# Opening each ConvFFN of a two-layer decoder trunk with one pair of column tiles instead of two

## The chip, the cores and the metric

The kernel runs on one core of a Trainium2 chip, as one launch. The metric is the device time of one execution in microseconds; the median of three runs is given. The engines are TensorE (PE, with its weight loads as PEld), VectorE (DVE), ScalarE (ACT), GpSimd (POOL) and SyncE (SP), which here issues the DMAs.

## The reference

A hybrid decoder trunk of two layers on an input of 256 rows by 1024 columns, float32. Layer 0 adds an mLSTM mixer, layer 1 a block-sparse attention over a shared K and V; each layer then adds a ConvFFN, and this is what the change touches:

```python
def conv_ffn(x, norm_g, w_up, conv_w, conv_b, w_down):
    s_ = x.shape[1]
    u = rmsnorm(x, norm_g) @ w_up                 # 1024 -> 2 * 2816
    up = jnp.pad(u, ((0, 0), (CONV_W - 1, 0), (0, 0)))
    c = conv_b + up[:, 0:s_] * conv_w[0]
    for j in range(1, CONV_W):                    # three taps along the sequence
        c = c + up[:, j:j + s_] * conv_w[j]
    val, gate = jnp.split(c, 2, axis=-1)
    return (jax.nn.silu(gate) * val) @ w_down

# each layer:  h = h + mixer(h);  h = h + conv_ffn(h, ...)
# rmsnorm(x, g) = x * rsqrt(mean(x * x) + 1e-6) * g
```

## The kernel before

The activations are held transposed: hT is eight tiles of 128 columns of the model by 256 rows of the sequence. Each float32 product is built from high and low parts: a weight unit of 128 x 2048 is loaded by SP into raw (three buffers), copied by ACT into hi and subtracted by DVE into lo, in two halves each (`unit`, L164 to L174; hi and lo have four buffers each). The operands are split alike; `xa` holds the gain-scaled tiles of hT, high part and low part side by side.

A step of `steps_w` (L227) is one slice k of 128 model columns into one column tile of the output: one matmul of the unit's low part on the operand's high part (256 columns, L246), and one of the unit's high part on both parts of the operand (512 columns, L242). The result stands in one of five PSUM accumulators (`acc`); it has two halves of 256 columns, which `whole` (L279) adds together with an ACT copy and a DVE addition.

What runs before a ConvFFN is `project_out` (L298): eight output tiles n, and with the last step of each, `residual` (L289) adds both halves of the accumulator to hT[n] (L290, L292) and `feed` splits hT[n] into xa[n] (L181 on ACT, L182 on DVE) and adds its squares to `sqacc` (L199 on ACT, L200 on POOL, for the last tile on DVE). So the operands of the ConvFFN appear one by one, and the sum of squares behind the last.

The up projection has 22 pairs of column tiles: pair i is the value tile and the gate tile i, and has one weight unit, so 16 steps. The normalisation factor of a row is not known before all eight tiles of hT are. Pairs 0 to 2 (`DEFER`) therefore run on the unnormalised operand xa and are multiplied by the factor afterwards; from pair 3 on the operand is xb, which `rescale` builds from hT and the factor: for each k a product xs on DVE (L349, four buffers), its high part on ACT (L351) and its low part on POOL (L352). `Rstd.sums` adds sqacc over the partitions on PE (L213), then DVE and POOL make the factor (L215, L217); `Rstd.row`, the first thing in `rescale`, spreads it over the partitions by two PE transposes (L222) and an ACT copy into rB (L224).

PE's instructions keep the order in which they are written. The other engines' are put in order by a planner as their operands and buffers come free. `mix` (L69) writes PE steps in their order and puts an item between them as soon as the steps before it have a summed cost of at least the item's number; a step counts 0.32:

```python
def mix(steps, items=()):
    items, now = list(items), 0.0
    for cost, step in steps:
        while items and items[0][0] <= now:
            items.pop(0)[1]()
        step()
        now += cost
```

Before, the opening mixes pairs 0 and 1: for each k, four steps, two for each pair. The sums (5.0) stand after 16 of its 32 steps, the rescaling (6.6) after 21. Then `finish(0)` and `finish(1)` evacuate both pairs, convolve (L323, L327, L330) and gate them, and from pair 2 on each pair runs its 16 steps (all k of one half, then of the other) and is finished.

Of the kernel before, what the change touches and what calls it, by code (L numbers as in the profile page):

```python
# [21 lines left out]
KD = D // P  # L22
NT = S // P
FF = 2816
KF = FF // P
# [8 lines left out]
BIG = 1e30  # L34
L = 2
DEFER = 3
AHEAD = 2
GROUP = 4
HOLD = 4
WARM = 8  # L40
# [28 lines left out]
# [8 lines that stand above are left out]
    for _, item in items:  # L77
        item()
# [3 lines left out]
def yoco_kernel(ctx: ExitStack, tc: tile.TileContext, A, out):  # L82
# [23 lines left out]
    for j in range(4):  # L106
        c = slice(j * 512, (j + 1) * 512)
        nc.sync.dma_start(raw0[:, c], A["w_kq"][0, :, c])
        if j < 3:
            k = slice(2 * j + 2, 2 * j + 4)  # L110
# [16 lines left out]
    for j in range(WARM):  # L127
        ps = pmis.tile([P, 512], F32, name="mis")
# [35 lines left out]
    def unit(src, length, raw=None, pieces=PIECES):  # L164
        if raw is None:
            raw = wraw.tile([P, 2048], F32, name="raw")[:, :length]
            nc.sync.dma_start(raw, src)
        hi = wsp.tile([P, 2048], F32R, name="hi")[:, :length]
        lo = wsp.tile([P, 2048], F32R, name="lo")[:, :length]
        for j in range(pieces):  # L170
            c = slice(j * length // pieces, (j + 1) * length // pieces)
            nc.scalar.activation(hi[:, c], raw[:, c], AF.Copy)  # L172
            nc.vector.tensor_tensor(lo[:, c], raw[:, c], hi[:, c].bitcast(F32), OP.subtract)  # L173
        return hi, lo  # L174
# [11 lines left out]
    def operand(pool, name, n):  # L186
        ts = [pool.tile([P, 2 * S], F32R, name=f"{name}{k}") for k in range(n)]
        return [t[:, :S] for t in ts], [t[:, S:] for t in ts], ts
# [38 lines left out]
    def steps_w(ps, w, at, x, ks, kall, done=None, apart=True):  # L227


        xh, xl, both = x  # L230

        def one(k):
            (hi, lo), p = w(), ps()
            c = slice(at(k), at(k) + P)
            last = k == kall - 1

            def high():
                if not apart:
                    for n, xs in enumerate((xh, xl)):
                        nc.tensor.matmul(p[:, :S], hi[:, c], xs[k], start=k == 0 and n == 0, stop=last and n == 1)  # L240
                    return
                nc.tensor.matmul(p, hi[:, c], both[k], start=k == 0, stop=last)  # L242

            if k == 0:
                high()
            nc.tensor.matmul(p[:, :S], lo[:, c], xh[k], start=False, stop=False)  # L246
            if k > 0:
                high()
            if last and done is not None:
                done(p)  # L250

        return [(0.32, lambda k=k: one(k)) for k in ks]
# [26 lines left out]
    def whole(ps, rows=P):  # L279

        y = work.tile([P, S], F32, name="whole", bufs=WHOLE)[:rows]
        nc.scalar.activation(y, ps[:rows, S:], AF.Copy)  # L282
        nc.vector.tensor_tensor(y, ps[:rows, :S], y, OP.add)  # L283
        return y
# [4 lines left out]
    def residual(n, ps, gains, apart=True):  # L289
        nc.vector.tensor_tensor(hT[:, n], ps[:, :S], hT[:, n], OP.add)  # L290
        if apart:
            nc.vector.tensor_tensor(hT[:, n], ps[:, S:], hT[:, n], OP.add)  # L292
        if gains is None:
            nc.sync.dma_start(out[:, n, :], hT[:, n])
        else:
            feed(n, gains)
# [16 lines left out]
    def conv_ffn(l, gains):  # L313
        r = Rstd()
        with tc.tile_pool(name=f"ffn{l}", bufs=1, reuse_waits="tile") as fp, \
                tc.tile_pool(name=f"ffw{l}", bufs=2, reuse_waits="tile") as fw:
            act = operand(fp, "f", KF)
            ah, al, _ = act

            def conv(ps, c, scaled):  # L320
                u = whole(ps)
                if not scaled:
                    nc.vector.tensor_tensor(u, u, r.rB, OP.mult)  # L323
                w = [par[:, C_CW + (l * 3 + j) * 2 * KF + c:][:, :1] for j in range(3)]
                b = par[:, C_CB + l * 2 * KF + c:][:, :1]
                y = fw.tile([P, S], F32, name="y", bufs=4)
                nc.scalar.activation(y, u, AF.Identity, bias=b, scale=w[2])  # L327
                for j in (1, 0):
                    d = 2 - j
                    nc.vector.scalar_tensor_tensor(y[:, d:], u[:, :S - d], w[j], y[:, d:],  # L330
                                                   op0=OP.mult, op1=OP.add)
                return y

            def finish(i, ps):
                y = [conv(ps[half](), half * KF + i, i >= DEFER) for half in range(2)]
                sg = fw.tile([P, S], F32, name="sg", bufs=2)
                nc.scalar.activation(sg, y[1], AF.Silu)  # L337
                a = fw.tile([P, S], F32, name="a", bufs=2)
                nc.gpsimd.tensor_tensor(out=a, in0=sg, in1=y[0], op=OP.mult)  # L339
                nc.scalar.activation(ah[i], a, AF.Copy)  # L340
                nc.gpsimd.tensor_tensor(out=al[i], in0=a, in1=ah[i].bitcast(F32), op=OP.subtract)  # L341

            def rescale():

                r.row()
                g0 = C_FNORM + l * KD
                for k in range(KD):
                    xs = fw.tile([P, S], F32, name="xs", bufs=4)
                    nc.vector.scalar_tensor_tensor(xs, hT[:, k], par[:, g0 + k:g0 + k + 1], r.rB,  # L349
                                                   op0=OP.mult, op1=OP.mult)  # L350
                    nc.scalar.activation(setB[0][k], xs, AF.Copy)  # L351
                    nc.gpsimd.tensor_tensor(out=setB[1][k], in0=xs, in1=setB[0][k].bitcast(F32), op=OP.subtract)  # L352

            def pair(i, ks):
                x = setA if i < DEFER else setB
                return [s for half in range(2)
                        for s in steps_w(ps[i][half], w[i], lambda k, half=half: k * 256 + half * P, x, ks, KD)]

            w = [Once(lambda i=i: unit(A["w_up"][l, i], 2048)) for i in range(KF)]
            ps = [[Once(acc) for half in range(2)] for i in range(KF)]  # L360

            mix([s for k in range(KD) for i in range(AHEAD) for s in pair_k(pair, i, k)],
                [(5.0, r.sums), (6.6, rescale)])
            for i in range(AHEAD):
                finish(i, ps[i])
            for i in range(AHEAD, KF):
                mix(pair(i, range(KD)))
                finish(i, ps[i])

            wd = [Once(lambda i=i: unit(A["w_down"][l, i], 11 * P)) for i in range(2 * KD)]  # L370
            pd = [Once(acc) for n in range(KD)]

            def down(n, ks):
                apart = gains is not None or n < KD - 1
                return [s for k in ks for s in
                        steps_w(pd[n], wd[2 * n + k // 11], lambda q: (q % 11) * P, act, [k], KF,
                                lambda p: residual(n, p, gains, apart), apart)]


            for ks in (range(KF // 2), range(KF // 2, KF)):  # L380
                for n in range(HOLD):
                    mix(down(n, ks))
            for n in range(HOLD, KD):
                mix(down(n, range(KF)))

    def pair_k(pair, i, k):
        return pair(i, [k])


    wgv = wgs.rearrange("p (k m) -> p k m", k=KD)  # L390
# [12 lines left out]
    with tc.tile_pool(name="mls", bufs=1, reuse_waits="tile") as mp, \  # L403
            tc.tile_pool(name="mlw", bufs=2, reuse_waits="tile") as mw:
        r = Rstd()
# [199 lines left out]
    for i in range(2):  # L605
# [3 lines left out]
        for a in range(2):  # L609
            ha, hb = slice(a * HALF, (a + 1) * HALF), slice((1 - a) * HALF, (2 - a) * HALF)  # L610
            nc.gpsimd.tensor_tensor(out=tab[:, i, :, 1, ha], in0=rope[:, :, 1, ha], op=OP.mult,  # L611
                                    in1=g[:, None, hb].to_broadcast([P, NT, HALF]))

    conv_ffn(0, [(C_KVNORM, setA), (C_BNORM, setB)])


    with tc.tile_pool(name="att", bufs=1, reuse_waits="tile") as mp, \
            tc.tile_pool(name="atw", bufs=2, reuse_waits="tile") as mw:
        r = Rstd()
# [105 lines left out]
        project_out(A["w_o"], setB, [(C_FNORM + KD, setA)], [it(1.0 + 0.6 * h, values, 4 + h) for h in range(4)])  # L725

    conv_ffn(1, None)


# [68 lines left out]
```

## Time and profile before

| what | value |
|---|---|
| median of 3 runs | 602.32 us (602.27 to 602.56) |
| the profiled execution's own time | 602.21 us |
| its span, first to last instruction | 600.5 us |
| PE busy in the span | 591.0 us (98%) |
| DVE busy | 495.4 us (82%) |
| ACT busy | 393.0 us (65%) |
| POOL busy | 172.7 us (29%) |
| mean granted TensorE clock | 0.996 of full speed |

The profile is of one execution. Its span leaves out what lies before the first and behind the last instruction, 1.7 us here. Busy is the time in which an engine has an instruction under way; matmuls overlap, and their ends are modelled, so the starts are what counts for PE. The first ConvFFN starts at about 115.9 us of the span, the second at about 410.2 us.

### The profile page before, as it was taken

How to read it: one execution, taken by the hardware profiler on the slowest of the kernel's cores; microseconds unless marked ns; L12 is line 12 of the kernel's file. 1: busy time of each engine (PE TensorE's matmuls, PEld its weight loads, DVE VectorE, ACT ScalarE, POOL GpSimd, SP SyncE). 2: the span in 40 equal slices, each digit the busy share in tenths (PEclk: the TensorE clock that was granted, in tenths of full speed). 3: DMA queues.
4: the chain of work that ended last, by engine and by line, in shares of the span. 5: the costliest groups of instructions: out<-in, count | busy, mean ns of one | idle time of the engine just before them, and what ended most of it. 6: DMA issues, size and time to landing. Idle time of an engine off the chain costs nothing.

```text
span 600.5 us, 8992 instructions
## 1 busy us (share of the span) xinstructions
PE 591.0 (98%) x3278; PEld 504.8 (84%) x3278; DVE 495.4 (82%) x837; ACT 393.0 (65%) x713; POOL 172.7 (29%) x186
## 2 busy tenths in 40 slices
PE   7899999999999999999999999999999999999997
PEld 4787888888888888888888878888888888888887
DVE  7897677979999999988768786467999999998650
ACT  5756776667886777765656687554878767676430
POOL 6600310343545344301111200022545453432000
PEclk8999999999999999999999999999999999999999
DMA  7874434617445543486755533335364456346830
GB/s 245 309 269 181 141 140 141 211 70 255 167 151 200 199 139 136 151 266 203 246 204 185 200 120 139 129 138 214 106 228 158 153 198 209 103 141 209 265 110 19
DMA packets 18621, 105.79 MB, mean 176 GB/s; under 512 B 2320, under 2 KB 3856, under 8 KB 9104
## 3 DMA queue, kind: packets, MB, share of 16 engines
q1 hardware_dynamic: 18576, 105.21, 50.0%
q8 instruction: 26, 0.43, 0.3%
q14 instruction: 19, 0.16, 0.1%
HBM read 104.15 MB, written 1.05 MB: 175 GB/s over the span
## 4 chain that ended last, share of the span: by engine, by line
PE 87%; DVE 6%; ACT 3%; POOL 2%; issue 1%; DMA 1%; SPq 0%; DVEq 0%; POOLq 0%
PE acc L242 41%; PE acc L246 21%; PE acc L263 6%; PE acc L265 6%; PE acc L264 6%; DVE lo L173 3%; ACT hi L172 1%; DVE xs L349 1%; DVE xa L182 1%; PE acc L240 1%; DMA hT<-xT 1%; PE mis L551 1%; POOL tab L611 1%; DVE hT L292 1%; PE mis L666 1%
## 5 line engine op out<-in xcount | busy, mean ns | idle before, releaser
L173 DVE TENSOR_TENSOR lo<-raw,hi 128x1024 fp32r<-128x1024 f32 (+2 forms) x218 | 247.5, 1165 | 28.9 <-ACT hi L172 28.6
L242 PE MATMUL acc<-xb,hi 128*128 128x512 f32 x736 | 252.3, 396 | 0.6 <-POOL xb L352 0.6
L172 ACT ACTIVATE hi<-raw 128x1024 fp32r<-128x1024 f32 (+2 forms) x218 | 199.8, 964 | 56.1 <-PE acc L242 25.4
L246 PE MATMUL acc<-xb,lo 128*128 128x256 f32 x736 | 191.3, 279 | 0.0
L242 PEld LDWEIGHTS acc<-xb,hi 128*128 128x128 f32 x736 | 131.8, 188 | 26.2 <-POOL xb L352 1.2
L246 PEld LDWEIGHTS acc<-xb,lo 128*128 128x128 f32 x736 | 138.7, 188 | 8.0
L242 PE MATMUL acc<-f,hi 128*128 128x512 f32 x330 | 115.0, 394 | 0.0
L330 DVE SCALAR_TENSOR_TENSOR y<-whole,par,y 128x254 f32<-128x254 f32 (+1 forms) x176 | 110.2, 645 | 3.2 <-ACT y L327 2.8
L246 PE MATMUL acc<-f,lo 128*128 128x256 f32 x352 | 96.8, 282 | 0.0
L339 POOL TENSOR_TENSOR a<-sg,y 128x256 f32<-128x256 f32 x44 | 58.7, 1333 | 97.6 <-ACT sg L337 97.6
L242 PEld LDWEIGHTS acc<-f,hi 128*128 128x128 f32 x330 | 61.1, 188 | 13.0
L246 PEld LDWEIGHTS acc<-f,lo 128*128 128x128 f32 x352 | 66.1, 188 | 1.3
L327 ACT ACTIVATE y<-whole,par 128x256 f32<-128x256 f32 x88 | 51.7, 595 | 20.8 <-DVE whole L283 18.8
L242 PE MATMUL acc<-xa,hi 128*128 128x512 f32 x160 | 57.4, 402 | 0.9 <-DVE hT L292 0.5
L263 PE MATMUL acc<-hi,xa 128*128 128x512 f32 x128 | 53.3, 417 | 0.0
L341 POOL TENSOR_TENSOR f<-a,f 128x256 fp32r<-128x256 f32 x44 | 42.3, 962 | 36.3 <-ACT f L340 36.3
L265 PE MATMUL acc<-hi,xa 128*128 128x512 f32 x128 | 50.1, 391 | 0.0
L264 PE MATMUL acc<-lo,xa 128*128 128x512 f32 x128 | 50.0, 391 | 0.0
L200 POOL TENSOR_TENSOR sqacc<-sqacc,sq 128x256 f32<-128x256 f32 x18 | 16.4, 910 | 115.2 <-ACT sq L199 115.2
L246 PE MATMUL acc<-xa,lo 128*128 128x256 f32 x160 | 44.3, 289 | 0.5 <-DVE lo L173 0.5
L283 DVE TENSOR_TENSOR whole<-acc,whole 128x256 f32<-128x256 f32 (+1 forms) x97 | 39.4, 412 | 0.0
L282 ACT ACTIVATE whole<-acc 128x256 f32<-128x256 f32 (+1 forms) x97 | 35.4, 368 | 5.8 <-PE acc L242 5.7
(180 smaller groups left out, 638.2 us busy)
## 6 DMA issues: line engine op xcount, KB each, us to landing
raw<-w_up SPq DMA_DIRECT2D x44, 1024.0 KB, 4.8
raw<-w_down SPq DMA_DIRECT2D x32, 704.0 KB, 4.7
raw<-w_kqv SPq DMA_DIRECT2D x12, 1024.0 KB, 4.8
raw<-w_vo SPq DMA_DIRECT2D x8, 1024.0 KB, 4.9
raw<-w_out SPq DMA_DIRECT2D x4, 1024.0 KB, 4.9
raw<-w_o SPq DMA_DIRECT2D x4, 1024.0 KB, 4.8
raw<-w_kq SPq DMA_DIRECT2D x2, 1024.0 KB, 7.8
raw<-w_kq SPq DMA_DIRECT2D x4, 256.0 KB, 5.4
```

The lines of the kernel that those rows point to most:

```text
L172: nc.scalar.activation(hi[:, c], raw[:, c], AF.Copy)
L173: nc.vector.tensor_tensor(lo[:, c], raw[:, c], hi[:, c].bitcast(F32), OP.subtract)
L242: nc.tensor.matmul(p, hi[:, c], both[k], start=k == 0, stop=last)
L246: nc.tensor.matmul(p[:, :S], lo[:, c], xh[k], start=False, stop=False)
L263: nc.tensor.matmul(p, xh[k][:, ts], hi[:, c], start=k == 0, stop=False)
L264: nc.tensor.matmul(p, xh[k][:, ts], lo[:, c], start=False, stop=False)
L265: nc.tensor.matmul(p, xl[k][:, ts], hi[:, c], start=False, stop=k == KD - 1)
L283: nc.vector.tensor_tensor(y, ps[:rows, :S], y, OP.add)
L327: nc.scalar.activation(y, u, AF.Identity, bias=b, scale=w[2])
L330: nc.vector.scalar_tensor_tensor(y[:, d:], u[:, :S - d], w[j], y[:, d:], op0=OP.mult, op1=OP.add)
L339: nc.gpsimd.tensor_tensor(out=a, in0=sg, in1=y[0], op=OP.mult)
L341: nc.gpsimd.tensor_tensor(out=al[i], in0=a, in1=ah[i].bitcast(F32), op=OP.subtract)
```

## The change

The opening takes pair 0 alone, slice by slice: two steps for each k. The sums stand after 14 of these 16 steps. Pair 1 runs behind them, one half after the other as later pairs do, with the rescaling after three of its steps. The constant AHEAD and the function `pair_k` go; everything else stays.

```diff
-AHEAD = 2
...
-            mix([s for k in range(KD) for i in range(AHEAD) for s in pair_k(pair, i, k)],
-                [(5.0, r.sums), (6.6, rescale)])
-            for i in range(AHEAD):
-                finish(i, ps[i])
-            for i in range(AHEAD, KF):
-                mix(pair(i, range(KD)))
+            mix([s for k in range(KD) for s in pair(0, [k])], [(4.2, r.sums)])
+            mix(pair(1, range(KD)), [(0.7, rescale)])
+            for i in range(KF):
+                if i > 1:
+                    mix(pair(i, range(KD)))
                 finish(i, ps[i])
...
-    def pair_k(pair, i, k):
-        return pair(i, [k])
```

## Rows read from the trace of the kernel before

**Rows 1.** The page, part 1: busy time, share, instructions of PE.

```profile
PE 591.0 (98%) x3278; PEld 504.8 (84%) x3278; DVE 495.4 (82%) x837; ACT 393.0 (65%) x713; POOL 172.7 (29%) x186
```

**Rows 2.** Waits of PE, whole span: us in total, times, longest us.

```profile
PE acc L242 <- POOL xb L352: 0.6, 2, 0.3
PE acc L242 <- DVE hT L292: 0.5, 2, 0.3
```

**Rows 3.** Timeline of PE, first opening: start us, us, what, idle time before and releaser.

```profile
115.89 0.40 PE L242 MATMUL acc<-xa,hi 128*128 128x512 f32 x1
...
117.37 0.47 PE L242 MATMUL acc<-xa,hi 128*128 128x512 f32 x1 [0.27 <-DVE hT L292]
...
118.27 0.39 PE L242 MATMUL acc<-xa,hi 128*128 128x512 f32 x1
...
121.73 0.39 PE L242 MATMUL acc<-xa,hi 128*128 128x512 f32 x1
122.01 0.61 PE L213 MATMUL mis<-tri,sqacc 128*128 128x1 f32 x4
122.47 0.37 PE L246 MATMUL acc<-xa,lo 128*128 128x256 f32 x1
...
124.30 0.38 PE L222 MATMUL mis<-ident,rc 128*128 128x128 f32 x2
```

**Rows 4.** Timeline of ACT, first opening.

```profile
116.09 2.01 ACT L172 ACTIVATE hi<-raw 128x1024 fp32r<-128x1024 f32 x2 [1.30 <-PE acc L242]
118.00 0.49 ACT L181 ACTIVATE xa<-hT,par 128x256 fp32r<-128x256 f32 x1
...
118.71 0.49 ACT L181 ACTIVATE xa<-hT,par 128x256 fp32r<-128x256 f32 x1
...
124.72 0.39 ACT L224 ACTIVATE rB<-mis 128x256 f32<-128x256 f32 x1 [5.20 <-PE mis L222]
```

**Rows 5.** Timeline of DVE, first opening.

```profile
117.93 2.90 DVE L173 TENSOR_TENSOR lo<-raw,hi 128x1024 fp32r<-128x1024 f32 x2
120.75 0.87 DVE L182 SCALAR_TENSOR_TENSOR xa<-hT,par,xa 128x256 fp32r<-128x256 f32 x2
121.54 0.41 DVE L200 TENSOR_TENSOR sqacc<-sqacc,sq 128x256 f32<-128x256 f32 x1
...
125.14 3.93 DVE L349 SCALAR_TENSOR_TENSOR xs<-hT,par,rB 128x256 f32<-128x256 f32 x6 [2.33 <-ACT rB L224]
```

**Rows 6.** Chain that ended last, from rescaling to pair 3: start us, us, what.

```profile
128.91 1.89 ACT hi L172 x2
130.80 0.28 ACT whole L282
...
131.66 1.90 ACT hi L172 x2
...
133.85 0.98 ACT y L327 x2
...
135.22 1.72 POOL xb L352
```

**Rows 7.** Timeline of PE, eighth step of pair 3, first and second ConvFFN.

```profile
136.98 0.72 PE L242 MATMUL acc<-xb,hi 128*128 128x512 f32 x2 [0.33 <-POOL xb L352]
...
431.33 0.73 PE L242 MATMUL acc<-xb,hi 128*128 128x512 f32 x2 [0.29 <-POOL xb L352]
```

**Rows 8.** Timelines of POOL and DVE, first rescaling.

```profile
126.15 4.22 POOL L352 TENSOR_TENSOR xb<-xs,xb 128x256 fp32r<-128x256 f32 x5 [2.55 <-ACT xb L351]
...
135.13 2.88 DVE L173 TENSOR_TENSOR lo<-raw,hi 128x1024 fp32r<-128x1024 f32 x2
```

**Rows 9.** Stretch after the rescaling: us, busy us of engines, PE clock, DMA share, GB/s.

```profile
137.00:240.00 103.00, 103.00 (x589) 89.77 (x590) 101.32 (x156) 76.96 (x147) 45.45 (x38) 1.00 0.50 178
```

**Rows 10.** Timeline of DVE, second opening.

```profile
412.29 2.90 DVE L173 TENSOR_TENSOR lo<-raw,hi 128x1024 fp32r<-128x1024 f32 x2
415.11 0.87 DVE L182 SCALAR_TENSOR_TENSOR xa<-hT,par,xa 128x256 fp32r<-128x256 f32 x2
```

## Prediction

> **What bounds the kernel now.** I read the page first: PE is busy for 591.0 of 600.5 us [rows 1], so only a PE wait that comes or goes can move the end. Then PE's waits: in the whole span two kinds belong to the opening of a ConvFFN, each 0.3 us and each seen twice, once per ConvFFN [rows 2]. All that the change can take away is therefore about 1.1 us. Next came PE's timeline through the first opening, to place these waits and to get the price of a step; then the timelines of ACT and DVE over the same microseconds, to see when the last operands are written; then the chain of work from the sums to pair 3, and last the second ConvFFN.
>
> A step is one 128-row slice k into one column tile: a 256-column and a 512-column matmul. From 118.27 to 121.73 PE starts 11 consecutive 512-column matmuls, so ten steps take 3.46 us, 0.346 us each [rows 3]. Steps 1 to 16 run from 115.89 with a 0.27 us wait before step 4, which needs the fourth accumulator of five while tile 6 of the projection is still held by its residual add. The sums (L213) follow at 122.01, step 17 at 122.47, the transposes of the factors (L222) at 124.30, five steps after the sums [rows 3].
>
> The operands: ACT writes the high parts of xa[6] and xa[7] at 118.00 and 118.71, after both halves of the weight unit for pair 3 at 116.09 [rows 4]. DVE takes that unit's two subtractions first, 117.93 to 120.83, and only then the low parts of xa[6] and xa[7] (120.75, 0.87 us for both) and the last addition into sqacc (121.54, 0.41 us) [rows 5]. So xa[6] is whole at about 121.2, xa[7] at 121.6, sqacc at 121.95. Before the change nobody feels this: the opening reaches k = 6 after 24 steps, beyond the sums, and the sums come when sqacc has just been written.
>
> From the sums a chain runs past PE: factors, xs on DVE, xb high on ACT, xb low on POOL. In it ACT does two more weight units (1.89 and 1.90 us) and two convolution activations (0.98 us) before the last xb [rows 6]. The last POOL subtraction ends at 136.94, and PE, which wanted it for the eighth step of pair 3, waits 0.33 us; 0.29 us in the second ConvFFN [rows 6, 7]. After that PE has no wait to the end of the up projection.
>
> **The change, part by part.**
>
> *One pair instead of two in the opening.* No instruction is added or removed; 16 steps of pair 1 move from between the steps of pair 0 to behind them. Removed: the 0.27 us wait before step 4, since two accumulators are wanted while three are free. Added: k now advances every 2 steps, not 4. Step 13 is the first with k = 6, and PE gets there at 115.89 + 12 x 0.346 = 120.04. It must wait for xa[6] until about 121.2 (only the small matmul, which reads the high part alone, can go ahead). With the 0.1 us that PE took after its other wait, steps 13 and 14 run from 121.3 to 122.0. So PE gains a wait of about 1.2 us on DVE.
>
> *Sums sooner.* They stand in front of step 15 instead of step 17 (14 x 0.32 = 4.48 is the first sum over 4.2). But they need sqacc, which comes at 121.95 as before: they start at 122.0, not sooner. This is the crux: at the same instant PE has done 14 steps where it had done 16. The loss is 2 x 0.346 = 0.69 us, the old wait before step 4 already counted.
>
> *Rescaling sooner.* 0.7 is passed after three steps of pair 1, so the transposes stand after 2 + 3 = 5 steps from the sums, as before (16 to 21). They start at 124.30 again, and xs starts at 125.14 at the earliest.
>
> *Pair 3.* Its eighth step needs the last xb. Before, PE was ready for it at 136.98 - 0.33 = 136.65; now at 136.65 + 0.69 = 137.34. If the last xb still comes at 136.94, the 0.33 us wait (0.29 in the second) is gone, hidden behind PE's delay. Net loss: 0.69 - 0.33 = 0.36 and 0.69 - 0.29 = 0.40 us.
>
> *The order behind it.* Pair 0 ends at 122.47 + 2 x 0.346 = 123.2 instead of 122.47 + 14 x 0.346 = 127.3, so its accumulators and its weight buffer come free earlier. ACT, idle for 5.20 us until 124.72 [rows 4], and DVE, idle for 2.33 us until 125.14 [rows 5], may take pair 0's evacuation and the weight unit of pair 4 at once. Once begun, that holds up the factors: two evacuations of 0.28 us and two halves of 0.95 us (1.89 / 2) on ACT [rows 6] from about 123.0 end at 125.5, and DVE's two subtractions, at 1.45 us each [rows 5], run up to about 127.0. So xs starts between 125.14 and 127.0. In return one of the two units (1.89 us of ACT) leaves the chain behind it. The bounds of the last xb are then 136.94 - 1.9 = 135.0 (nothing delayed, a unit gone) and 136.94 + 1.9 = 138.8 (all delayed, nothing given back), against 137.34, when PE wants it: a new wait between nothing and 1.5 us per ConvFFN. I take nothing, because the two shifts are the same work moved from behind the start of xs to ahead of it, which leaves the last xb near 136.9.
>
> The Trainium skill ("SBUF — State Buffer", Who interferes with whom) says that a VectorE instruction with two SBUF inputs and a GpSimd one that reads SBUF block each other fully, the later waiting for the earlier. Here the last POOL subtraction took 1.72 us beside a weight subtraction on DVE, against 4.22 / 5 = 0.84 us in the run of five [rows 6, 8]: longer by 0.88 us, but less than the 1.44 us (2.88 / 2) of the piece beside it, so slowed and not wholly blocked. By the rule to the letter the last xb would come at about 135.13 + 1.44 + 0.84 = 137.4, and the sum would grow by less than 0.1 us per ConvFFN.
>
> *Weights, DMA, the rest.* The weight units of pairs 0 to 2 are split before the opening needs them; their loads keep their order, and buffers come free no later. DVE is busy for 101.32 of 103 us in the stretch after 137 [rows 9], without PE waiting there; work pulled forward into DVE's 2.33 us gap only relieves it. Cost nothing.
>
> **Sum.** The second ConvFFN repeats the first (subtractions at 412.29, low parts at 415.11) [rows 10]. Total + 0.36 + 0.40 = + 0.76 us. On the profiled execution, 602.21 us: 602.97. The median of the runs shown is 602.32, 0.11 higher, so 603.1 us, 0.13% more. With the bounds: 0.76 + 2 x 1.5 = 3.8 us at most from late rescaling, 606.1.
>
> **Rivals.**
>
> *Operands in time (faster).* DVE could take the two low parts behind the first half of the weight unit, at 117.93 + 1.45 = 119.4, when both high parts are written or nearly so. Then xa[7] is whole at 120.2 and sqacc at 120.6, and 14 steps end at 115.89 + 14 x 0.346 = 120.73: the sums start 1.28 us sooner with 0.69 us less work done, a gain of 0.59, and the 0.3 us wait for the last xb goes as well. 0.9 us per ConvFFN, 600.5 us. It decides from the point at which xa[6] is whole by 120.0. For it: PE's new need might pull the order. Against it: both ConvFFNs show the same order [rows 5, 10], the unit is released by the projection's last tile, ahead of the opening, and the diff touches nothing that DVE or ACT gets before xa[7]. 14%.
>
> *Rescaling late (slower).* The weight unit of pair 4 goes ahead of the factors, and the chain doesn't get the time back, since xs, with four buffers, ACT and POOL pass on every hitch. Half of its bound, 0.75 us per ConvFFN: 603.1 + 1.5 = 604.6. It decides once the last xb is over 0.6 us later than before. For it: ACT's idle stretch lies exactly where the unit becomes possible. Against it: one unit fewer behind. 22%.
>
> *Waits that only change places (the change does nothing).* If the projection's end lets DVE run some 0.4 us sooner, or the chain shortens so that PE's delay is all that counts, loss and gain cancel within 0.4 us: 602.3. 10%.
>
> **How the numbers follow.** My forecast has 54%, 602.6 to 603.5. A measurement of this kernel can tell about 0.2%, 1.2 us, from no change: under 601.1 is faster, over 603.5 slower. The first rival is all faster, with 2% for an unforeseen order: 16%. The second is nearly all slower, and of the forecast some 8% lie just over the line: 29%. The rest is the same: 55%. For the range, from 600.8 (most of the first rival outside) to 604.8 (the second up to its middle and a little over) leaves out under 2 in 10.
>
> **What would show it.** PE's waits after: no residual add before step 4; a new one on the low part of xa (L182) of about 1.2 us, twice, in the opening; sums again at about 6.1 us from the opening's start; no wait on POOL's xb in pair 3, which starts 0.69 us later. On DVE the two weight subtractions still stand ahead of the last low parts. Wrong would be: the low parts ahead of a weight subtraction (faster), or a wait on xb in pair 3 longer than 0.3 us (slower).

## The result, and the profile after

The changed kernel takes 606.81 us (median of 6 runs, 606.18 to 607.08) against 602.44 us for the kernel before on the same chips: 1.0069 times as long, 95% interval 1.0058 to 1.0080. It is slower by 4.4 us, where 0.8 us was forecast.

Of PE's waits over the whole span, these two the change made or enlarged (columns as in [rows 2]; the line numbers are one less than before, since a constant is gone):

```profile
PE acc L241 <- POOL xb L351: 2.5, 4, 1.0
PE acc L241 <- DVE xa L181: 1.7, 2, 0.9
```

The wait on the residual add is gone from the list, as forecast; the one on xa has come, twice; the one on xb, which was to vanish, has grown from 0.6 to 2.5 us. PE's timeline in the first ConvFFN places them (compare [rows 3, 7]):

```profile
116.94 0.40 PE L241 MATMUL acc<-xa,hi 128*128 128x512 f32 x1
...
122.26 0.49 PE L241 MATMUL acc<-xa,hi 128*128 128x512 f32 x1 [0.82 <-DVE xa L181]
...
122.99 0.60 PE L212 MATMUL mis<-tri,sqacc 128*128 128x1 f32 x4
...
125.30 0.38 PE L221 MATMUL mis<-ident,rc 128*128 128x128 f32 x2
...
139.02 0.50 PE L241 MATMUL acc<-xb,hi 128*128 128x512 f32 x1 [0.97 <-POOL xb L351]
139.89 0.73 PE L241 MATMUL acc<-xb,hi 128*128 128x512 f32 x2 [0.26 <-POOL xb L351]
```

The opening starts at 116.94. The sums come at 122.99, 6.05 us behind it, where it was 6.12 us before with two steps more done. That is the loss that was forecast. Then the seventh and the eighth step of pair 3 wait for POOL, together 1.23 us instead of 0.33. Why the last xb is late stands in the timelines of ACT, DVE and POOL (compare [rows 4, 5, 8]):

```profile
124.10 0.73 ACT L281 ACTIVATE whole<-acc 128x256 f32<-128x256 f32 x2 [3.54 <-PE acc L241]
124.72 2.00 ACT L171 ACTIVATE hi<-raw 128x1024 fp32r<-128x1024 f32 x2
126.62 0.37 ACT L223 ACTIVATE rB<-mis 128x256 f32<-128x256 f32 x1
...
130.86 2.00 ACT L171 ACTIVATE hi<-raw 128x1024 fp32r<-128x1024 f32 x2
132.75 1.08 ACT L326 ACTIVATE y<-whole,par 128x256 f32<-128x256 f32 x2
133.74 0.71 ACT L350 ACTIVATE xb<-xs 128x256 fp32r<-128x256 f32 x2
...
136.73 0.42 ACT L350 ACTIVATE xb<-xs 128x256 fp32r<-128x256 f32 x1 [0.28 <-DVE xs L348]
```

```profile
118.89 2.92 DVE L172 TENSOR_TENSOR lo<-raw,hi 128x1024 fp32r<-128x1024 f32 x2
121.73 0.87 DVE L181 SCALAR_TENSOR_TENSOR xa<-hT,par,xa 128x256 fp32r<-128x256 f32 x2
122.52 0.41 DVE L199 TENSOR_TENSOR sqacc<-sqacc,sq 128x256 f32<-128x256 f32 x1
...
125.81 2.36 DVE L172 TENSOR_TENSOR lo<-raw,hi 128x1024 fp32r<-128x1024 f32 x2 [0.52 <-ACT hi L171]
128.08 2.15 DVE L348 SCALAR_TENSOR_TENSOR xs<-hT,par,rB 128x256 f32<-128x256 f32 x4
130.16 1.84 DVE L322 TENSOR_TENSOR whole<-whole,rB 128x256 f32<-128x256 f32 x2
...
134.27 1.21 DVE L172 TENSOR_TENSOR lo<-raw,hi 128x1024 fp32r<-128x1024 f32 x1
135.40 0.41 DVE L322 TENSOR_TENSOR whole<-whole,rB 128x256 f32<-128x256 f32 x1
135.74 0.96 DVE L348 SCALAR_TENSOR_TENSOR xs<-hT,par,rB 128x256 f32<-128x256 f32 x1
136.62 1.76 DVE L172 TENSOR_TENSOR lo<-raw,hi 128x1024 fp32r<-128x1024 f32 x1
```

```profile
129.10 3.51 POOL L351 TENSOR_TENSOR xb<-xs,xb 128x256 fp32r<-128x256 f32 x4 [4.51 <-ACT xb L350]
134.22 5.62 POOL L351 TENSOR_TENSOR xb<-xs,xb 128x256 fp32r<-128x256 f32 x4 [1.62 <-ACT xb L350]
```

The ACT rows show the reversal: evacuation of pair 0, both halves of pair 4's weight unit, and only then the copy of the factor into rB, which PE's transposes had made possible at about 125.7 (they start 2.31 us behind the sums and take 0.38). DVE does the unit's two subtractions before the first xs. So xs starts 128.08 - 122.99 = 5.09 us behind the sums, 3.13 before (125.14 - 122.01). From there to the end of the last POOL subtraction it takes 139.84 - 128.08 = 11.76 us, 11.80 before (136.94 - 125.14).

The table puts together, for each kernel's profiled execution (the other kernels are the experiments of the next section), four distances in the first ConvFFN, in us, each a difference of two starts in the timelines (the third to the end of the last POOL subtraction). By rounding, a last digit can be off by one. The last column is what PE's end hangs on: from the first step of the opening to the 512-column matmul of the eighth step of pair 3.

| kernel | opening to sums | sums to xs | xs to last xb | opening to step 8 of pair 3 |
|---|---|---|---|---|
| before | 6.12 | 3.13 | 11.80 | 21.09 |
| changed | 6.05 | 5.09 | 11.76 | 22.95 |
| e3_sooner | 6.11 | 3.13 | 10.47 | 21.32 |
| e1_hold | 6.06 | 3.13 | 12.27 | 21.51 |
| e2_unit4 | 6.06 | 3.13 | 9.57 | 21.28 |
| e10_unit5 | 6.06 | 5.10 | 10.68 | 21.89 |
| e11_conv | 6.12 | 5.09 | 9.19 | 21.34 |
| e5_unit3 | 4.94 | 4.99 | 11.47 | 21.45 |
| e6_both | 4.94 | 3.53 | 12.28 | 20.81 |
| e7_ms | 4.94 | 3.33 | 12.27 | 20.60 |
| e8_two | 4.94 | 3.55 | 9.62 | 20.36 |
| e9_pairs | 6.08 | 3.33 | 9.31 | 20.80 |

In the second ConvFFN the last column is 21.10 before and 23.03 after, so the two openings lose 1.86 + 1.93 = 3.8 us. The profiled spans differ by 605.4 - 600.5 = 4.9 us; the other 1.1 lie ahead of the first opening, which starts at 116.94 and not at 115.89 (last section).

### The profile page after: what moved, and what is told of

Its sections match the earlier page's. It is cut to its first block, busy times and chain, and to the rows that moved or that the text cites. A ratio compares the mean times of both kernels' runs of the same rounds, so it can differ in the third digit from the quotient of the medians.

```text
span 605.4 us, 8972 instructions
## 1 busy us (share of the span) xinstructions
PE 593.3 (98%) x3278; PEld 506.1 (84%) x3278; DVE 497.4 (82%) x837; ACT 392.2 (65%) x713; POOL 172.4 (28%) x186
## 3 DMA queue, kind: packets, MB, share of 16 engines
HBM read 104.15 MB, written 1.05 MB: 174 GB/s over the span
## 4 chain that ended last, share of the span: by engine, by line
PE 89%; issue 5%; POOL 3%; ACT 1%; DVE 1%; DMA 1%; SPq 0%; POOLq 0%; DVEq 0%
PE acc L241 42%; PE acc L245 22%; PE acc L262 6%; PE acc L264 6%; PE acc L263 6%; POOL xb L351 2%; PE acc L239 1%; DMA hT<-xT 1%; ACT hi L171 1%; PE mis L546 1%; PE mis L661 1%; PE acc L673 1%; PE mis L689 0%; DVE sqacc L395 0%; PE acc L671 0%
## 5 line engine op out<-in xcount | busy, mean ns | idle before, releaser
L329 DVE SCALAR_TENSOR_TENSOR y<-whole,par,y 128x255 f32<-128x255 f32 (+1 forms) x176 | 108.9, 638 | 5.0 <-ACT y L326 4.5
L338 POOL TENSOR_TENSOR a<-sg,y 128x256 f32<-128x256 f32 x44 | 57.3, 1301 | 98.2 <-ACT sg L336 98.1
```

## The experiments

Each time below is a median of 11 or 12 runs, set against the kernel before on the same chip; the ratio has its 95% interval beside it. The added lines shift the line numbers in some of the rows.

Orders are added with a helper that lets the planner place one instruction only behind another of the same engine; it moves no data and adds no instruction:

```python
def behind(late, early):
    tc.add_manual_dep(late.ins, early.ins.name, mybir.DependencyInfo(
        mybir.DependencyClass.NoSync, mybir.DependencyReason.DATA), reason="order")
```

`unit` got two arguments for it, `hi_after` for its ACT copies and `lo_after` for its DVE subtractions; `r.last` is the ACT copy of the last xb, `r.xs` the last xs, `r.ms` DVE's small operation behind the sums, `tail` the last addition into sqacc.

**Freeing pair 0 as late as before (e1_hold).**

```diff
-            mix([s for k in range(KD) for s in pair(0, [k])], [(4.2, r.sums)])
-            mix(pair(1, range(KD)), [(0.7, rescale)])
+            one, two = [s for k in range(KD) for s in pair(0, [k])], pair(1, range(KD))
+            mix(one[:14] + two[:12] + one[14:] + two[12:], [(4.2, r.sums), (5.8, rescale)])
```

> The changed kernel, but pair 0's last two steps (k = 7) stand behind 12 steps of pair 1, nine steps behind the transposes, so that pair 0's accumulators and the weight buffer for pair 4 come free as late as they did before. PE has the same steps, the sums stay after 14. Theory: some 1.2 us per ConvFFN of the slowdown come from pair 4's weight unit and pair 0's evacuation going ahead of the factor copy, which starts xs 2 us later. Then xs starts 3.1 us after the sums again (not 5.1), the last xb is there 15 us after them, the wait in pair 3 is gone, the wait on xa[6] of 0.8 us stays, and the time is that of before plus 0.7 to 0.9 us, about 603.2. Rival: the late xb comes from running pair 1 behind pair 0 whatever frees when (pair 1's evacuation and unit fall on xs): the wait in pair 3 stays near 1 us and the time within 0.5 us of the changed kernel, 606 to 607.

Measured: 603.69 us against 602.62, ratio 1.0018 (1.0006 to 1.0031). xs starts 3.13 us behind the sums, the last xb is there 15.4 us behind them, the wait on xb is gone from PE's list, and PE still waits for xa, 1.7 us in the two openings. The theory holds: step 8 of pair 3 comes 1.44 us sooner than in the changed kernel, so of the 4.4 us some 3 come from what pair 0's early end lets in. The chain is still just late: step 8 starts 0.05 us behind the end of the last POOL subtraction (138.31 and 138.26), and 0.23 us later than in e2_unit4.

**Pair 4's weight unit alone (e2_unit4).**

```diff
-            w = [Once(lambda i=i: unit(A["w_up"][l, i], 2048)) for i in range(KF)]
+            w = [Once(lambda i=i: unit(A["w_up"][l, i], 2048, hi_after=(lambda: r.last) if i == 4 else None))
+                 for i in range(KF)]
```

> The changed kernel, with one order added: the ACT copies of pair 4's weight unit go behind the last xb copy of the same ConvFFN. Pair 0's evacuation stays early. If the weight unit alone makes the last xb late: xs starts 3.1 to 3.5 us after the sums, the wait in pair 3 goes, the time is 603.0 to 603.6. If pair 0's evacuation and convolution, which now fall into the rescaling, do it: xs starts early but the last xb still comes over 16 us after the sums, a wait of over 0.7 us stays in pair 3 and the time is over 605.

Measured: 602.84 us against 602.62, ratio 1.0002 (0.9993 to 1.0011). The planner put pair 5's unit behind the last xb along with it. On POOL the eight subtractions now take 8.57 us from the first start to the last end, 10.74 in the changed kernel (timeline of POOL):

```profile
126.30 3.51 POOL L359 TENSOR_TENSOR xb<-xs,xb 128x256 fp32r<-128x256 f32 x4 [2.55 <-ACT xb L358]
130.62 1.68 POOL L359 TENSOR_TENSOR xb<-xs,xb 128x256 fp32r<-128x256 f32 x2 [0.81 <-ACT xb L358]
133.12 1.75 POOL L359 TENSOR_TENSOR xb<-xs,xb 128x256 fp32r<-128x256 f32 x2 [0.81 <-ACT xb L358]
```

The last ends at 134.87, 2.5 us before PE wants it. Pair 0's evacuation and convolution stay early here (its multiplications again stand behind four xs, at 127.37) and cost PE nothing. One order, which moves two units, takes nearly the whole slowdown away: step 8 is 0.19 us later than before. What is left is the two steps lost at the sums.

**Sums and rescaling sooner, two pairs as before (e3_sooner).**

```diff
-                [(5.0, r.sums), (6.6, rescale)])
+                [(4.2, r.sums), (5.8, rescale)])
```

> The kernel before, opening with two pairs, with the numbers of the changed one alone: sums after 14 of its steps, rescaling after 19. Theory: the sums cannot come sooner than sqacc, so PE waits for it with two steps less behind it, 0.4 to 0.7 us per ConvFFN; pair 0 still ends late, so the weight unit for pair 4 stays behind the factor, xs starts 3.1 us after the sums and the wait in pair 3 goes: net 0.2 to 0.4 us each, 602.8 to 603.4. Rival (sooner sums help by themselves): faster than before by 0.3 to 0.6 us.

Measured: 602.89 us against 602.55, ratio 1.0008 (0.9999 to 1.0017). PE's waits show the price of sums that stand ahead of what they read:

```profile
PE mis L213 <- DVE sqacc L200: 1.2, 2, 0.6
```

The sums start 6.11 us behind the opening, as before, and step 8 of pair 3 comes 0.23 us later. This half of the change is worth a loss of 0.2 us per ConvFFN, a little over half of what the forecast gave the whole; the gain that the rival expected did not come.

**What ate the time that the chain should have got back (e10_unit5, e11_conv).** In the changed kernel one weight unit fewer lies between xs and the last xb, and yet the stretch is as long as before. The first of these two puts pair 5's unit behind the last xb; the second puts the multiplications of pairs 0 and 1 by the factor behind the last xs:

```diff
-            w = [Once(lambda i=i: unit(A["w_up"][l, i], 2048)) for i in range(KF)]
+            w = [Once(lambda i=i: unit(A["w_up"][l, i], 2048, hi_after=(lambda: r.last) if i == 5 else None))
+                 for i in range(KF)]
```

> The changed kernel, with ACT's copies of pair 5's weight unit behind the last xb copy; pair 4's unit still goes ahead of the factor copy, so xs still starts 5.1 us after the sums. From the start of xs to the last xb the changed kernel takes 11.76 us, as before the change (11.79), although one unit fewer lies in between. If units are what the chain is short of time for: 9.6 us, as with pair 4's unit (and with it pair 5's) behind the last xb; the last xb comes 14.7 us after the sums, the wait in pair 3 goes, 602.9 to 603.6. If not the unit but the convolution of pairs 0 and 1 fills the chain: over 11 us, over 605.

```diff
                 if not scaled:
-                    nc.vector.tensor_tensor(u, u, r.rB, OP.mult)
+                    m = nc.vector.tensor_tensor(u, u, r.rB, OP.mult)
+                    if not scaled:
+                        behind(m, r.xs)
```

> The changed kernel, with DVE's multiplications of pairs 0 and 1 by the factor (and so their convolutions) behind the last xs; both weight units stay where the change has them. If it is this work that took the place of the unit that left the chain: xs to the last xb falls from 11.76 to about 10 us, the last xb comes 15.0 to 15.4 us after the sums and the wait in pair 3 all but goes, 603.0 to 603.8. If the chain is as long without it: 11.3 us or more, and the wait in pair 3 stays over 0.7 us, 605.5 or more.

Measured: 604.29 us (ratio 1.0022, 1.0011 to 1.0033) and 603.28 us (1.0005, 0.9994 to 1.0016), against 602.81. Without pair 5's unit the stretch from xs to the last xb is 10.68 us, between the two answers expected (9.6 and over 11), and PE waits 0.4 us for xb in each ConvFFN. With the unit but without the convolutions it is 9.19 us, shorter than expected, and PE doesn't wait for xb. Timelines of POOL, DVE and ACT in the second:

```profile
128.46 3.52 POOL L357 TENSOR_TENSOR xb<-xs,xb 128x256 fp32r<-128x256 f32 x4 [4.51 <-ACT xb L356]
132.61 4.04 POOL L357 TENSOR_TENSOR xb<-xs,xb 128x256 fp32r<-128x256 f32 x4 [0.63 <-ACT xb L356]
```

```profile
133.32 0.96 DVE L354 SCALAR_TENSOR_TENSOR xs<-hT,par,rB 128x256 f32<-128x256 f32 x1
134.21 3.06 DVE L326 TENSOR_TENSOR whole<-whole,rB 128x256 f32<-128x256 f32 x4
137.19 1.22 DVE L176 TENSOR_TENSOR lo<-raw,hi 128x1024 fp32r<-128x1024 f32 x1
```

```profile
130.23 2.00 ACT L175 ACTIVATE hi<-raw 128x1024 fp32r<-128x1024 f32 x2
132.13 1.02 ACT L356 ACTIVATE xb<-xs 128x256 fp32r<-128x256 f32 x3
```

xs still starts 5.09 us behind the sums. So the late start alone costs PE nothing: the chain does get its time back, if nothing else takes it. What took it was the convolution work together with pair 5's unit; without either the stretch is shorter, most of all without the convolutions. Pair 0's early evacuation had made its part of them ready. In the changed kernel it stands on DVE between the fourth xs and the last (130.16, 1.84 us) and on ACT in front of the fifth copy of xb (132.75, 1.08 us).

The 2.57 us that e11_conv takes out of the stretch have two parts. Its fifth POOL subtraction starts 0.99 us sooner behind the first xs (132.61 - 127.46 = 5.15 us; 134.22 - 128.08 = 6.14 in the changed kernel), since ACT goes from the unit straight to the copies. And its last four subtractions take 4.04 us instead of 5.62. The order holds back the multiplications of pairs 0 and 1 and the ACT work that reads them, and DVE's second weight subtraction then falls behind POOL's end as well (137.19, and 132.61 + 4.04 = 136.65); how much is pair 0's alone was not tried.

**The operand in time (e5_unit3), and both repairs (e6_both).** DVE's two subtractions of pair 3's unit go behind the last addition into sqacc; the second kernel has the held-back steps of e1_hold as well.

```diff
-            w = [Once(lambda i=i: unit(A["w_up"][l, i], 2048)) for i in range(KF)]
+            tail = last[0]
+            w = [Once(lambda i=i: unit(A["w_up"][l, i], 2048, lo_after=(lambda: tail) if i == 3 else None))
+                 for i in range(KF)]
```

> The changed kernel, with one order added: DVE's two subtractions of pair 3's weight unit go behind the last addition into sqacc. Theory: the wait on xa[6] (0.8 us) is DVE's order alone; it goes, the sums start 1.2 us sooner relative to the opening, and the whole chain behind them too. The late start of xs (5.1 us after the sums) stays, as pair 4's unit still goes ahead. PE gains 0.85 us and some 0.3 us of the wait in pair 3, per ConvFFN: 606.8 - 2.3 = 604.5. Rival: the two subtractions now stand right in front of the small DVE operation behind the sums and hold the factor up by what was won: the wait in pair 3 grows by about 0.8 us and the time stays over 606.

> The two repairs together: pair 0's last steps held back as in the first of these kernels, and DVE's subtractions of pair 3's unit behind sqacc. Theory: no wait on xa, none on xb; against before PE loses neither the 0.27 us on the accumulator nor the 0.3 us on xb, and the sums come sooner: 602.4 - 1.2 = 601.2, between 600.6 and 601.8. Rival: two steps fewer before the sums only move the wait, 602.4 within 0.4.

Measured: 603.79 us (1.0008, 0.9994 to 1.0022) and 602.32 us (0.9992, 0.9983 to 1.0000), against 602.62. The wait on xa goes in both, and the sums start 4.94 us behind the opening, 1.1 us sooner. In e5_unit3, where pair 4's unit stays early, PE still waits for xb, 0.9 us in four waits. e5_unit3 came out under both of its answers (604.5, and over 606), but the rival's mechanism is there. e6_both, expected at 601.2, came out where its rival stood (602.4). DVE's timeline in e5_unit3:

```profile
120.08 0.41 DVE L209 TENSOR_TENSOR sqacc<-sqacc,sq 128x256 f32<-128x256 f32 x1
120.42 2.35 DVE L176 TENSOR_TENSOR lo<-raw,hi 128x1024 fp32r<-128x1024 f32 x2
122.69 0.15 DVE L224 TENSOR_SCALAR ms<-mis 128x2 f32<-128x2 f32 x1
```

The small operation behind the sums, ready some 1 us earlier, stands behind 2.35 us of subtractions, and PE waits for the factor at the transposes: 0.3 us in each ConvFFN, in both kernels. In e6_both step 8 also starts only 0.05 us behind the end of the last POOL subtraction, so the late chain still sets it.

**The order moved once more (e7_ms), without held-back steps (e8_two), and on two pairs (e9_pairs).** The subtractions go behind the small operation:

```diff
-            w = [Once(lambda i=i: unit(A["w_up"][l, i], 2048)) for i in range(KF)]
+            w = [Once(lambda i=i: unit(A["w_up"][l, i], 2048, lo_after=(lambda: r.ms) if i == 3 else None,
+                                       hi_after=(lambda: r.last) if i == 4 else None)) for i in range(KF)]
```

e7_ms has the first of the two orders and the steps of e1_hold; e8_two has both orders and the steps of the change; e9_pairs has both orders and the steps of the kernel before.

> One pair in the opening, pair 0's last steps held back, and DVE's subtractions of pair 3's unit behind the small DVE operation of the factor, not only behind sqacc. In the kernel with both repairs PE waited 0.3 us for the factor at the transposes, as the subtractions stood before that operation. Theory: this wait goes and the chain starts 0.35 us sooner: the eighth step of pair 3 comes 20.4 to 20.5 us after the opening (20.81 there), 0.6 us sooner than before per ConvFFN: 601.2. Rival: the subtractions now fall on xs and hold it up by as much: no difference from the kernel with both repairs.

> One pair in the opening as in the change, no step held back, and two orders: DVE's subtractions of pair 3's unit behind the small operation of the factor, ACT's copies of pair 4's unit behind the last xb copy. Theory: all waits of PE between the opening and pair 3 go; the eighth step of pair 3 comes 20.1 us after the opening (21.1 before), 1.0 us sooner per ConvFFN: 600.5, 0.3% faster than before. Rival: weight units pushed back make PE wait for pair 4's or 5's weights: a new PE wait on lo or hi near 140 us, and no gain.

> The kernel before, two pairs in its opening, with the same two orders. If the orders are what is worth something and one pair or two is not: within 0.3 us per ConvFFN of the kernel with one pair and both orders, 600.5 to 601.3. If the opening with one pair is worth more than the 0.27 us of the accumulator wait (sums two steps sooner once the operand is there): slower than that one by over 0.3 us per ConvFFN, 601.3 to 602.2.

Measured against 602.55 us: e7_ms 602.04 (0.9986, 0.9978 to 0.9995), e8_two 601.04 (0.9972, 0.9963 to 0.9981), e9_pairs 601.89 (0.9994, 0.9981 to 1.0007). In e7_ms the wait for the factor is gone and step 8 comes 0.21 us sooner than in e6_both, but it still starts 0.05 us behind the last POOL subtraction (137.62 and 137.57); with the held-back steps the stretch from xs to the last xb is 12.27 us, 9.62 without them in e8_two. In e8_two PE has no listed wait at all from the first opening to the end of its up projection. DVE's timeline there:

```profile
118.97 0.48 DVE L189 SCALAR_TENSOR_TENSOR xa<-hT,par,xa 128x256 fp32r<-128x256 f32 x1 [0.53 <-ACT xa L188]
119.67 0.73 DVE L189 SCALAR_TENSOR_TENSOR xa<-hT,par,xa 128x256 fp32r<-128x256 f32 x1 [0.22 <-ACT xa L188]
120.32 0.41 DVE L207 TENSOR_TENSOR sqacc<-sqacc,sq 128x256 f32<-128x256 f32 x1
121.81 0.16 DVE L222 TENSOR_SCALAR ms<-mis 128x2 f32<-128x2 f32 x1 [1.07 <-PE mis L220]
121.88 1.22 DVE L176 TENSOR_TENSOR lo<-raw,hi 128x1024 fp32r<-128x1024 f32 x1
```

xa and sqacc are done 1.6 us earlier, counted from the opening (120.73 - 116.33 = 4.4 us; 122.93 - 116.94 = 6.0 us in the changed kernel), and the weight subtractions fill the time in which DVE would wait for the factor. The kernel with one pair and both orders is some 5.8 us faster than the change as it was made, and 1.5 us faster than the kernel before, where 2 us was expected. Against two pairs with the same orders it gains 20.80 - 20.36 = 0.44 us per ConvFFN: the opening with one pair is worth something when xa[6] and xa[7] come in time. Where they come late, in e2_unit4, it loses 0.19 us against the kernel before.

## Why the prediction was wrong

**Right, with its size.** The accumulator wait went. PE got a wait on xa[6], 0.82 and 0.9 us where 1.2 was worked out; the 512-column matmul of step 13 starts 5.32 us behind the opening's start (122.26 - 116.94), forecast 5.4, and the small matmul that goes ahead counts as busy. DVE kept its order, both subtractions ahead of the low parts. The sums did not come sooner, 6.05 us behind the opening where 6.1 was forecast, and two steps fewer were done: pair 3 starts 12.65 us behind the sums, 11.94 before, 0.71 us for the forecast 0.69. In e2_unit4 and e11_conv, which take the late chain away, the forecast's other terms come out in kind and somewhat smaller: 0.19 and 0.25 us more to step 8 of pair 3 (forecast 0.36). Their times, 602.84 and 603.28 us, are 0.2 and 0.5 us above the kernel before on the same chip, neither clear of noise, where 0.8 was forecast.

**The step that failed** is the last part of "The order behind it": "I take nothing, because the two shifts are the same work moved from behind the start of xs to ahead of it, which leaves the last xb near 136.9". The same goes for the sentence that work pulled forward into DVE's gap "only relieves it". The first shift was right to the tenth: xs at 128.08 with the opening 1.05 us later, so 127.03 on the old scale, against a bound of 127.0. The second did not come: the stretch from xs to the last xb stayed at 11.76 us. The last xb is 1.9 us later, the upper bound of 138.8 itself (139.84 - 1.05 = 138.79), and the price by that bound is 0.36 + 1.5 = 1.86 us, just the 1.86 measured. That it fits to the hundredth is luck: without the late chain the loss is 0.19 to 0.25 us, so the late chain cost 1.6 to 1.7. The bounds of the last xb held; the choice between them did not. The prediction's own sign for slower came, a wait on xb in pair 3 longer than 0.3 us. The measured 606.8 lies even above its bound of 606.1, since the two openings explain 3.8 us of the 4.4; in the profiled executions the rest lies ahead of the first opening (last section).

The late start of xs is pair 4's unit: with it held back, and the evacuation as early as in the changed kernel, xs starts 3.13 us behind the sums (e2_unit4). The reason that was missed is the other half: pair 0's evacuation goes ahead along with the unit, so that its convolution is ready as soon as the factor is. Its multiplications by the factor stand behind four of the eight xs in the changed kernel; in DVE's timeline of before they start at 130.57, behind seven. e11_conv shows that this work is needed for the loss: with the convolutions of pairs 0 and 1 moved back, the chain shortens by 2.6 us (11.76 to 9.19) and PE doesn't wait for xb. It is not enough by itself: without pair 5's unit the stretch is 1.1 us shorter (e10_unit5), and in e2_unit4, where the convolution is as early and both units are held back, it is 9.57. The order on pair 4's unit, which takes pair 5's along, or that on the convolutions is enough by itself; that on pair 5's is not quite.

**The rivals.** "Rescaling late" was the one that happened, priced at half its bound, 0.75 us per ConvFFN, and given 22%; it came with the whole. "Operands in time" did not happen of itself, but its figure is near what the order is worth: it gave 0.9 us per ConvFFN, and e8_two, with the order on pair 4's unit as well, has 0.73 (21.09 - 20.36). "Waits that only change places" did not happen.

**The port.** The Trainium skill's rule that a VectorE instruction with two SBUF inputs and a GpSimd instruction that reads SBUF block each other ("SBUF — State Buffer", Who interferes with whom) bears on the last four POOL subtractions, 5.62 us in the changed kernel, 4.04 in e11_conv, and 1.68 + 1.75 in e2_unit4. Taken singly, the fifth starts at 134.22, DVE's weight subtraction of 1.21 us at 134.27, and the POOL one takes 2.19 us; in e10_unit5, with no weight subtraction beside it, it takes 0.80. The seventh takes 1.70 us beside the weight subtraction of 136.62. That agrees with the rule: 2.19 us is a little over the two one behind the other (1.21 + 0.80). Here it was the POOL one that took longer, though its start is shown 0.05 us ahead. It goes the other way as well: pair 0's two multiplications take 1.84 us on DVE beside POOL, and 0.75 us before, at 130.57, where POOL is idle.

This is part of the loss. POOL has no gap from 134.22 to the last xb at 139.84, while ACT's last copy of xb is done at 136.73 + 0.42 = 137.15, so at the end the chain hangs on POOL's pace. The forecast had read one such pair in the kernel before as "slowed and not wholly blocked" from a mean of two pieces, 1.44 us. The single weight subtraction there takes 1.21 us, from 135.13 to 136.34, and POOL's subtraction ends 0.60 us behind it; that does not speak against blocking. How much of the 1.9 us is this and how much is order was not separated further.

## What to carry to other kernels

Finishing a piece of work earlier is not free when a planner fills idle engines with whatever has come free: look at what the freed buffers let start, and whether an engine is then taken when the critical chain needs it for its next link. Where work moves from behind a chain to ahead of it, don't count the time as given back before you have asked what else has become ready to take the gap. And an item written sooner in PE's order gains nothing unless what it reads comes sooner; the cure here was two orders, on DVE and ACT, and only with them did the new order on PE gain.

## What the runs showed of the hardware

The first opening starts at 115.9 to 116.3 us in some profiled executions and at 116.8 to 117.2 in others, whatever was changed behind it. The stretch from 15 to 27 us of the kernel after (columns as in [rows 9]) shows what differs:

```profile
15.00:27.00 12.00, 10.33 (x51) 8.49 (x50) 9.53 (x18) 6.52 (x10) 8.95 (x12) 0.86 0.89 332
```

The mean granted clock is 0.86 there; in the same stretch of the kernel before it is 1.00, the upper level (2.4 GHz) throughout. In the kernel after it is 0.50, the lower level (1.2 GHz), from 21 to 23 us, behind a wait, and PE's timeline shows it in the pace of the matmuls:

```profile
20.34 0.81 PE L212 MATMUL mis<-tri,sqacc 128*128 128x1 f32 x4 [0.78 <-DVE sqacc L395]
...
23.28 0.63 PE L241 MATMUL acc<-xa,hi 128*128 128x512 f32 x1
...
24.29 0.40 PE L241 MATMUL acc<-xa,hi 128*128 128x512 f32 x1
```

A 512-column matmul takes 0.63 us at 23.28 and 0.40 again at 24.29, where the clock is 1.00 again. The same wait of 0.8 us for sqacc stands in the executions with 1.00, so what decides is not settled. All five executions with 0.86 (the changed kernel, e1_hold, e6_both, e7_ms, e10_unit5) open late, all seven with 1.00 early. That is 0.5 to 1.3 us, as much as many of the effects here; distances counted from the opening are free of it, and agree between the two ConvFFNs within 0.1 us. The kernel before shows something like it in its own runs: of the 33 beside e7_ms, e8_two and e9_pairs, the nine with a mean granted clock of 0.994 took 603.06 to 603.64 us, the eight with 1.000 took 602.20 to 602.76; in which stretch the clock was lower there is not shown. So the medians are not free of it, and a difference of a few tenths between two medians here says less than the distances do.
